# A two-layer encoder trunk on one core: weight splits held behind a norm, TensorE's own order kept at the end of an attention branch, and four weight splits of the second layer made ahead

## The chip, the cores and the metric

The kernel runs on one core of one Trainium2 chip. The metric is the device time of one execution in microseconds (us), the median over the runs. The engines are named as in the profile: PE is TensorE (PEld its weight loads), DVE is VectorE, ACT is ScalarE, POOL is GpSimd, SP is SyncE, which here only issues the weight transfers.

## The reference

`x` is 512 tokens of 1024 channels in float32. Two layers are computed; in each one

```python
h = hybrid_mixer(x, ...)                       # three branches A, B, C
x = layer_norm(ALPHA * x + h, ln1_g, ln1_b)
h = memory_cross_attention(x, mem, wq, wkv, wo)
x = layer_norm(ALPHA * x + h, ln2_g, ln2_b)
h = conv_ffn(x, w_up, conv_k, conv_b, w_down)  # gated MLP
x = layer_norm(ALPHA * x + h, ln3_g, ln3_b)
```

and the mixer is

```python
proj = x @ w_in                                # q, k, v of A and B, u and v of C, the gates
out_a = window_attention(...)                  # 8 heads of 64, banded
out_b = dense_block_attention(...)             # 8 heads of 64, all 512 keys
out_c = u * (W_s @ LN(v) + b)                  # C: spatial gating, u and v through gelu
gates = sigmoid(gate + b_gate)                 # 3 x 1024 channels
merged = sum over the branches of (branch @ w_branch) * gate
return merged @ w_mix_out
```

## The kernel before

**Products.** Each float32 operand of a projection is split into a high part (a copy to the type fp32r, `split_hi`, ACT, L132) and a low part (operand minus high part, `split_lo`, DVE, L137). A product is three matmuls, high by high, high by low and low by high (`mm3`, L143 to L145). `acc<-xT,w` is the form of most projections, with the transposed activations `xT` and a weight tile `w`.

**Weights.** The weights come in 292 transfers of 512 KB (`raw`, issued on SP in a fixed order). The class `Weights` splits each into a tile of the pool `w`, which has five slots (`N_WSLOT`). `pump` is called in and behind each step and starts a split as soon as `room` says that a slot is free: the one used five tiles before has had its last step. Tiles that `is_apart` names (the first two pairs of the MLP's up weights) have room of their own in a big tile, `upw`, and may be split from a step on that `W.open` gives.

**Steps and order.** `layer` appends steps in program order to a list. Afterwards they are run through one by one. A scheduler with a view over the whole program then decides in which order each engine gets its instructions; program order is a priority to it, no order. The steps of attention are urgent: they are written under a raised priority (`URGENT`). SP alone is under `tc.manual_schedule`, which keeps program order on the engines it names.

**Branch B.** Sixteen steps u = 0 to 15 (head u // 2, half u % 2 of the queries). I write S, T and PV for their three parts and S9.1 for the second of the two query blocks of step 9:

- S(u), `bS_step`: four matmuls `s<-Kt,Q` (L665), two for each query block; for each block the row maximum (DVE, L667), then the exponential into a slot of `ring` (ACT, L127); then a reciprocal (DVE, L672) and the scaling of both blocks (POOL, L674). `ring` has four slots for these, so S(u).1 writes where the transposes of T(u-2).1 read.
- T(u), `bT_step`: eight transposes `t<-ident,ring` (PE, L688), four a block; each block goes to `PTb` as a high part (ACT, L132) and a low part (DVE, L137).
- PV(u), `bPV_step`: eight matmuls `pv<-PTb,V` (L702). Behind an odd u the head's output is put together as `o` (ACT L127, then DVE L632), and behind each second head it is split into `brB` (ACT L132, DVE L137).

The program order is S(u), a filler, PV(u-2), T(u-1). A filler is a gate step (`gate_step`, 24 matmuls `acc<-xT,w`, then a tanh) or a branch projection (`br_step`, 12 matmuls `acc<-brA,w` or `acc<-brB,w`). In the program the fillers `fA` of branch A's gates and projections stand between the steps of B; those of branch B (`fB`) and the gates `gB[0]`, `gB[1]` stand behind them.

**Around the MLP's norm.** The cross-attention ends in `wo_step(0..3)`; each adds its half row to `x` (`residual`, L332, L335) and then the norm of a row block follows (`ln_finish`, L340 to L349), which `xT_step(t)` transposes (L323) and splits into `xT` (ACT L132, DVE L137). The first up projections (`up_half_step`, `pv<-xT,upw` and `acc<-xT,upw`) take them two row blocks at a time. At the end of a layer the same stands between `down_t_step(0..3)` and the next layer's `v_step`.

Of the kernel before, what the change touches and what calls it, by code (L numbers as in the profile page):

```python
# [11 lines left out]
F32R = mybir.dt.float32r  # L12
# [4 lines left out]
P = 128  # L17
# [6 lines left out]
NPAIR = 22  # L24
# [9 lines left out]
HALVED = (0, 1)  # L34
# [42 lines left out]
def encoder_kernel(ctx: ExitStack, tc: tile.TileContext, x_in, xt_in, mem_in, w_in, pp_in, ln_in, cln_in, ws_in, co_in, out):  # L77
# [27 lines left out]
    def acc_tile(n=512):  # L105
        return ps_acc.tile([P, 512], F32, tag="acc", name="acc")

    def pv_tile():
        return ps_pv.tile([P, 512], F32, tag="pv", name="pv")

    def s_tile():
        return ps_s.tile([P, 512], F32, tag="s", name="s")

    def t_tile(dt=F32):
        return ps_t.tile([P, 4, P], dt, tag="t", name="t")

    def big_tile(shape, dt, name):
        return big.tile(shape, dt, tag="big", name=name)

    def p_tile(shape=(P, 512), dt=F32, name="pt"):  # L120
        return sp.tile(list(shape), dt, tag="p", name=name)
# [42 lines left out]
    class Weights:  # L164
        def __init__(self):
            self.order, self.pos, self.last = [], {}, []
            self.raw, self.tiles, self.raw_order, self.sums = {}, {}, [], {}
            self.nl = self.ns = self.freed = self.nlo = 0
            self.late, self.done, self.first = [], set(), []
            self.slots, self.apart, self.open = [], {}, {}  # L170

        def plan(self, steps):
            for i, st in enumerate(steps):
# [72 lines left out]
                split_hi(t[:, 0, sl], r)  # L246
            return parts

        def is_apart(self, key):


            return key[1] == "up" and key[2] % NPAIR in HALVED

        def place(self, key):
            if not self.is_apart(key):
                self.slots.append(self.ns)
                return wpool.tile([P, 2, 1024], F32R, tag="w", name="w")
            l, i = key[0], key[2] % NPAIR
            if (l, i) not in self.apart:
                self.apart[l, i] = big_tile([P, 2, 2, 1024], F32R, "upw")  # L260
            return self.apart[l, i][:, key[2] // NPAIR]

        def room(self, step):
            key = self.order[self.ns]
            if self.is_apart(key):
                return step >= self.open[key[0]]
            n = len(self.slots)
            return n < N_WSLOT or self.last[self.slots[n - N_WSLOT]] <= step

        def pump(self, step):  # L270
            new = 0
            while self.ns < len(self.order) and self.room(step):
                self.split()
                new += 1
            while self.late and (len(self.late) > new or self.first[self.nlo] <= step + 1):
                self.late.pop(0)()
            while self.nl < len(self.raw_order) and self.nl < self.freed + self.ahead():
                self.load()
# [9 lines left out]
    W = Weights()  # L288
# [24 lines left out]
    def evac_T(dst_h, dst_l, ps):  # L313
        split_hi(dst_h, ps)
        split_lo(dst_l, ps, dst_h)

    def xT_step(t):
        def fn():
            for i in range(2):
                pt = t_tile()  # L320
                for j in range(4):
                    k = 4 * i + j
                    nc.tensor.transpose(pt[:, j, :], X[0][:, t, k * P:(k + 1) * P], ident)  # L323
                evac_T(xT[:, t, 0, 4 * i:4 * i + 4, :], xT[:, t, 1, 4 * i:4 * i + 4, :], pt)
            pump()
        return Step(fn)
# [3 lines left out]
    def residual(t, half, ps):  # L330
        xs = X[0][:, t, half * 512:(half + 1) * 512]
        nc.vector.scalar_tensor_tensor(out=xs, in0=xs, scalar=ALPHA, in1=ps, op0=ALU.mult, op1=ALU.add)  # L332
        if half == 0:
            ln_stats[t] = small.tile([P, 2, 6], F32, tag="bn", name="bn", bufs=4)
        nc.vector.bn_stats(out=ln_stats[t][:, half, :], in_=xs)  # L335
# [18 lines left out]
    def load_ln(l, i, tiles=None):  # L354
        if tiles is None:
            gb = kv_p.tile([P, 2, 2, 512], F32, tag="k", name="lngb")
            tiles = [[gb[:, j, hf, :] for hf in range(2)] for j in range(2)]
        for j in range(2):
            for hf in range(2):
                bcast_row(tiles[j][hf], ln_in[l, i, j, hf * 512:hf * 512 + 512].partition_broadcast(P))  # L360
        return tiles
# [16 lines left out]
    steps = []  # L378

    def add(fn, chunks=()):  # L380
        steps.append(Step(fn, chunks))

    def layer(l):
        K = lambda kind, c: (l, kind, c)
# [383 lines left out]
        def fillers(n, stage):  # L768
            f = []
            for m in range(8):  # L770
                f.append(gate_step(n, m))
                f.append(br_step(n, m, stage))
            return f
# [186 lines left out]
        def gs_make(k):  # L960
            g, v = g_view(k), gs_view(k)
            split_hi(v[:, 0, :], g)
            split_lo(v[:, 1, :], g, v[:, 0, :])
# [131 lines left out]
        def down_mm(half, c, t, ps):  # L1095
            w = W.get(K("down", half * 11 + c), 2, 512)
            sl = slice(t * P, (t + 1) * P)
            for j in range(2):
                k = 2 * c + j
                g = gs_view(k)  # L1100
                mm3(ps, g[:, 0, sl], g[:, 1, sl], w[:, 0, j, :], w[:, 1, j, :], k == 0, k == 2 * 11 - 1)
# [3 lines left out]
        def down_k_step(half, c):  # L1105
            def fn():
                if c == 0:
                    if half == 0:
                        R["dn", 0] = [s_tile(), s_tile(), pv_tile(), acc_tile()]
                        gt = kv_p.tile([P, DM], F32, tag="v", name="ln3g", bufs=2)  # L1110
                        bt = [p_tile(name="ln3b") for _ in range(2)]
                        R["ln"] = load_ln(l, 2, ([gt[:, :512], gt[:, 512:]], bt))
                    else:
                        R["dn", 1] = [acc_tile() for _ in range(2)] + [
                            t_tile().rearrange("p a b -> p (a b)") for _ in range(2)]
                if half == 0:
                    for k in range(2 * c + 2, min(2 * c + 4, NPAIR)):
                        gs_make(k)
                for t in range(NT):
                    down_mm(half, c, t, R["dn", half][t])  # L1120
                pump()
                if half == 0 and c == 10:
                    for t in range(NT):
                        residual(t, 0, R["dn", 0][t])
            return Step(fn, [K("down", half * 11 + c)])
# [19 lines left out]
        def st(s):  # L1145
            steps.append(s)
# [24 lines left out]
        fC, fA, fB = fillers(2, 0), fillers(0, 1), fillers(1, 2)  # L1171
        for nm, fl in (("a", fC), ("b", fA)):
            if nm == "b":
                st(q_step("b", 0))
                st(aT_step(15))
                st(q_step("b", 1))
                st(qT_step("b", 0))
                st(aPV_step(7))
                st(q_step("b", 2))
                st(qT_step("b", 1))  # L1180
                st(q_step("b", 3))
                st(qT_step("b", 2))
            for t in range(NT):
                st(kv_step(nm, t))
                if t == 0:
                    st(qT_step(nm, 3))
                else:
                    st(kT_step(t - 1))
            st(fl.pop(0))
            st(kT_step(3))  # L1190
            S_, T_ = (aS_step, aT_step) if nm == "a" else (bS_step, bT_step)
            for u in range(16):
                st(S_(u))
                if fl:
                    st(fl.pop(0))
                if nm == "a" and u >= 3 and u % 2 == 1:
                    st(aPV_step((u - 3) // 2))
                if nm == "b" and u >= 2:
                    st(bPV_step(u - 2))
                if u >= 1:  # L1200
                    st(T_(u - 1))
            for f in fl:
                st(f)
        gB = [f for f in fB[0::2]]
        pB = [f for f in fB[1::2]]
        fB = [gB[2]]
# [6 lines left out]
        st(bT_step(15))  # L1213
        st(gB[1])
        st(bPV_step(15))
        for f in fB[:6]:
            st(f)
        add(load_x)
        for f in fB[6:]:
# [29 lines left out]
        st(xS_step(3))  # L1249
        st(mv_step(1))  # L1250
        st(xT_att_step(2))
        W.open[l] = len(steps)
        st(xPV_step(0))
        st(xT_att_step(3))
        st(xPV_step(1))
# [9 lines left out]
        for i, (j, part) in enumerate(first):  # L1265
            st(up_half_step(j, part, 0))
            if i == 1:
                st(xT_step(2))
        st(xT_step(3))
        for t, (j, part) in enumerate(first):  # L1270
            st(up_half_step(j, part, 1))
# [12 lines left out]
        st(up_step(NPAIR - 1, 1))  # L1284
        for c in range(11):
            st(down_k_step(0, c))
        for c in range(11 - NTAIL):
            st(down_k_step(1, c))
        st(down_t_step(0))
# [8 lines left out]
    for l in range(NLAYER):  # L1298
        layer(l)
# [147 lines left out]
```

## Time and profile before

| | |
|---|---|
| median of 3 runs | 1813.61 us (1813.51 to 1814.2) |
| the profiled execution | 1813.72 us |
| its span, first to last instruction | 1811.8 us |
| mean granted TensorE clock | 0.993 of full |
| PE busy | 1773.7 us, 98% of the span |
| DVE busy | 1259.2 us, 69% |
| ACT busy | 826.5 us, 46% |
| POOL busy | 229.3 us, 13% |

The span is what the trace holds; 1.9 us lie around it. An engine's busy time is a mean over the whole kernel, so the stretches in which PE waits have to be looked for one by one.

### The profile page before, as it was taken

How to read it: one execution, taken by the hardware profiler on the slowest of the kernel's cores; microseconds unless marked ns; L12 is line 12 of the kernel's file. 1: busy time of each engine (PE TensorE's matmuls, PEld its weight loads, DVE VectorE, ACT ScalarE, POOL GpSimd, SP SyncE). 2: the span in 40 equal slices, each digit the busy share in tenths (PEclk: the TensorE clock that was granted, in tenths of full speed). 3: DMA queues.
4: the chain of work that ended last, by engine and by line, in shares of the span. 5: the costliest groups of instructions: out<-in, count | busy, mean ns of one | idle time of the engine just before them, and what ended most of it. 6: DMA issues, size and time to landing. Idle time of an engine off the chain costs nothing.

```text
span 1811.8 us, 25762 instructions
## 1 busy us (share of the span) xinstructions
PE 1773.7 (98%) x9928; PEld 1544.6 (85%) x9928; DVE 1259.2 (69%) x2092; ACT 826.5 (46%) x1426; POOL 229.3 (13%) x268
## 2 busy tenths in 40 slices
PE   8999999999999999999999999999999899999998
PEld 6888888878978999988788888888789799999886
DVE  6666856557687889983566668565575978889734
ACT  4355645532453555652133555455324435556510
POOL 1112423120110000000011124321201100000000
PEclk9999999999999999999999999999999999999999
DMA  6222221242430222353322222212333402223321
GB/s 237 94 70 72 70 93 57 64 142 93 158 119 22 94 82 106 115 171 98 102 102 95 92 71 71 82 59 82 124 115 122 128 24 93 95 84 136 134 90 47
DMA packets 51242, 176.73 MB, mean 98 GB/s; under 512 B 5680, under 2 KB 6192, under 8 KB 50864
## 3 DMA queue, kind: packets, MB, share of 16 engines
q1 hardware_dynamic: 44784, 158.86, 26.3%
q10 hardware_dynamic: 6336, 16.23, 2.6%
q8 instruction: 78, 1.28, 0.3%
q14 instruction: 44, 0.36, 0.1%
HBM read 170.87 MB, written 4.19 MB: 97 GB/s over the span
## 4 chain that ended last, share of the span: by engine, by line
PE 93%; DVE 5%; issue 1%; ACT 1%; DMA 0%; DVEq 0%; SPq 0%; ACTq 0%
PE acc L145 20%; PE acc L143 20%; PE acc L144 20%; PE t L1031 2%; PE t L1030 2%; PE t L1029 2%; PE pv L702 2%; PE acc L1031 2%; PE acc L1030 2%; PE acc L1029 2%; PE s L665 2%; DVE w L137 1%; PE t L688 1%; PE s L145 1%; PE s L144 1%; PE s L143 1%
## 5 line engine op out<-in xcount | busy, mean ns | idle before, releaser
L137 DVE TENSOR_TENSOR w<-raw,w 128x1024 fp32r<-128x1024 f32 (+1 forms) x332 | 387.8, 1178 | 222.2 <-ACT w L132 219.7
L132 ACT ACTIVATE w<-raw 128x1024 fp32r<-128x1024 f32 (+1 forms) x332 | 327.2, 995 | 416.3 <-PE acc L145 251.6
L143 PE MATMUL acc<-xT,w 128*128 128x512 f32 (+1 forms) x736 | 281.9, 384 | 0.0
L145 PE MATMUL acc<-xT,w 128*128 128x512 f32 (+1 forms) x736 | 281.6, 383 | 0.1
L144 PE MATMUL acc<-xT,w 128*128 128x512 f32 (+1 forms) x736 | 281.1, 382 | 0.0
L143 PE MATMUL acc<-w,xT 128*128 128x512 f32 (+1 forms) x432 | 156.0, 362 | 7.2 <-ACT w L132 6.7
L145 PEld LDWEIGHTS acc<-xT,w 128*128 128x128 f32 x736 | 138.4, 188 | 25.3 <-DVE w L137 0.5
L144 PEld LDWEIGHTS acc<-xT,w 128*128 128x128 f32 x736 | 138.6, 188 | 23.6
L143 PEld LDWEIGHTS acc<-xT,w 128*128 128x128 f32 x736 | 138.3, 188 | 23.3
L145 PE MATMUL acc<-w,xT 128*128 128x512 f32 (+1 forms) x432 | 156.7, 364 | 0.0
L144 PE MATMUL acc<-w,xT 128*128 128x512 f32 (+1 forms) x432 | 155.5, 361 | 0.5 <-DVE w L137 0.5
L297 POOL TENSOR_TENSOR rs<-ve,mhalf 128x1 f32<-128x1 f32 x32 | 29.7, 929 | 920.4 <-DVE ve L342 878.7
L143 PEld LDWEIGHTS acc<-w,xT 128*128 128x128 f32 x432 | 82.2, 190 | 19.3 <-ACT w L132 6.7
L144 PEld LDWEIGHTS acc<-w,xT 128*128 128x128 f32 x432 | 82.1, 190 | 12.9 <-DVE w L137 1.0
L145 PEld LDWEIGHTS acc<-w,xT 128*128 128x128 f32 x432 | 82.0, 190 | 11.5
L667 DVE TENSOR_REDUCE nm<-s 128x1 f32<-128x512 f32 x64 | 44.1, 688 | 63.9 <-PE s L665 63.8
L1031 PE MATMUL t<-S,w 128*128 128x256 f32 x288 | 81.5, 283 | 0.0
L1030 PE MATMUL t<-S,w 128*128 128x256 f32 x288 | 81.5, 283 | 0.0
L1029 PE MATMUL t<-S,w 128*128 128x256 f32 x288 | 81.5, 283 | 0.0
L600 POOL TENSOR_SCALAR ring<-ring,rsm 128x256 f32<-128x256 f32 (+1 forms) x64 | 41.8, 666 | 182.2 <-DVE rsm L598 142.2
L674 POOL TENSOR_SCALAR ring<-ring,rsm 128x512 f32<-128x512 f32 x64 | 44.5, 708 | 144.4 <-DVE rsm L672 131.0
L753 POOL TENSOR_TENSOR mg<-mg,ring 128x512 f32<-128x512 f32 x32 | 46.5, 1454 | 121.2 <-DVE ring L752 121.2
(308 smaller groups left out, 4401.7 us busy)
## 6 DMA issues: line engine op xcount, KB each, us to landing
raw<-in_w_dram SPq DMA_DIRECT2D x292, 512.0 KB, 3.6
lngb<-in_ln_dram ACTq DMA_DIRECT2D x16, 256.0 KB, 4.2
xraw<-in_xt_dram SPq DMA_DIRECT2D x4, 512.0 KB, 6.7
memr<-in_mem_dram ACTq DMA_DIRECT2D x2, 1024.0 KB, 4.8
x<-in_x_dram ACTq DMA_DIRECT2D x4, 512.0 KB, 7.4
x_keep<-x ACTq DMA_DIRECT2D x4, 512.0 KB, 2.6
x<-x_keep ACTq DMA_DIRECT2D x4, 512.0 KB, 5.0
out_dram<-x SPq DMA_DIRECT2D x8, 256.0 KB, 2.0
```

Of the source, the lines that this page charges most:

```text
L132: nc.scalar.activation(out, in_, AF.Copy, scale=scale)
L137: eng.tensor_tensor(out=out, in0=in_, in1=hi.bitcast(F32), op=ALU.subtract)
L143: nc.tensor.matmul(ps, lhsT=lh, rhs=rh, start=first, stop=False)
L144: nc.tensor.matmul(ps, lhsT=lh, rhs=rl, start=False, stop=False)
L145: nc.tensor.matmul(ps, lhsT=ll, rhs=rh, start=False, stop=last)
L600: nc.gpsimd.tensor_scalar(out=pr_t[qi], in0=pr_t[qi], scalar1=rs[:, qi:qi + 1], scalar2=0.0, op0=ALU.mult, op1=ALU.add)
L667: nc.vector.tensor_reduce(out=nm[:, qi:qi + 1], in_=ps, axis=AX.X, op=ALU.max, negate=True)
L674: nc.gpsimd.tensor_scalar(out=pr_t[qi], in0=pr_t[qi], scalar1=rs[:, qi:qi + 1], scalar2=0.0, op0=ALU.mult, op1=ALU.add)
L753: nc.gpsimd.tensor_tensor(out=mg, in0=mg, in1=tg, op=ALU.add)
L1029: nc.tensor.matmul(o, lhsT=wh, rhs=x(0, k), start=first and k == 0, stop=False, **f)
L1030: nc.tensor.matmul(o, lhsT=wh, rhs=x(1, k), start=False, stop=False, **f)
L1031: nc.tensor.matmul(o, lhsT=wl, rhs=x(0, k), start=False, stop=last and k == 3, **f)
```

## The change

The diff has three parts. First, `W.hold`: weight splits of the kinds `up` and `us` (the MLP's) that go to the five slots have no room before the step that stands at `xT_step(3)` in front of the MLP. Second, `pe_in_order`: from in front of S(14) of branch B until behind the second of `fB`, PE is under `manual_schedule` and so keeps program order there. Third, `apart_of` takes the place of `is_apart`: the four `v` weights of the second layer get room of their own too (the big tile is now called `wa`), and may be split from the step on at which the first layer's second down half begins.

```diff
-        def is_apart(self, key):
-            return key[1] == "up" and key[2] % NPAIR in HALVED
+        def apart_of(self, key):
+            l, kind, c = key
+            if kind == "up" and c % NPAIR in HALVED:
+                return (l, kind, c % NPAIR), c // NPAIR
+            if kind == "v" and l > 0:
+                return (l, kind, c // 2), c % 2
+            return None
...
         def room(self, step):
             key = self.order[self.ns]
-            if self.is_apart(key):
-                return step >= self.open[key[0]]
+            if self.apart_of(key) is not None:
+                return step >= self.open[key[:2]]
+            if key[1] in ("up", "us") and step < self.hold[key[0]]:
+                return False
             n = len(self.slots)
...
+    def pe_in_order():
+        pe_order.append(tc.manual_schedule(engines={mybir.EngineType.PE}))
+        pe_order[-1].__enter__()
...
             for u in range(16):
+                if nm == "b" and u == 14:
+                    add(pe_in_order)
                 st(S_(u))
...
         st(bPV_step(15))
-        for f in fB[:6]:
+        for f in fB[:2]:
+            st(f)
+        add(pe_free)
+        for f in fB[2:6]:
             st(f)
...
-        W.open[l] = len(steps)
+        W.open[l, "up"] = len(steps)
...
+        W.hold[l] = len(steps)
         st(xT_step(3))
...
+        W.open[l + 1, "v"] = len(steps)
         for c in range(11 - NTAIL):
             st(down_k_step(1, c))
```

In the changed kernel L665 is L681, L688 is L704 and L702 is L718; the norm's lines stand seven lower (L332 is L339).

**PE in the middle of branch B, first layer.** Before, the scheduler has filled each round of S, PV and T with gate matmuls; this is the piece from S(14) on:

```order
L665 MATMUL s<-Kt,Q 128x512
L688 MATMUL t<-ident,ring 128x128
L665 MATMUL s<-Kt,Q 128x512
L688 MATMUL t<-ident,ring 128x128 x2
L145 MATMUL acc<-xT,w 128x512
L143 MATMUL acc<-xT,w 128x512
L144 MATMUL acc<-xT,w 128x512
L145 MATMUL acc<-xT,w 128x512
L143 MATMUL acc<-xT,w 128x512
L144 MATMUL acc<-xT,w 128x512
```

In the change, the same engine some rounds earlier, where S(12) and S(13) stand with T(10) and PV(9); the rows `s` are S, `t` are T, `pv` are PV:

```order
L681 MATMUL s<-Kt,Q 128x512 x2
L704 MATMUL t<-ident,ring 128x128 x4
L681 MATMUL s<-Kt,Q 128x512 x2
L718 MATMUL pv<-PTb,V 128x256 x6
L704 MATMUL t<-ident,ring 128x128
L718 MATMUL pv<-PTb,V 128x256
L704 MATMUL t<-ident,ring 128x128
L718 MATMUL pv<-PTb,V 128x256
L704 MATMUL t<-ident,ring 128x128 x2
L681 MATMUL s<-Kt,Q 128x512 x2
L704 MATMUL t<-ident,ring 128x128 x4
```

The matmuls `acc<-xT,w` have gone from these rounds: from S9.1 to S14.1 five rounds of 20 instructions each follow one another with no filler in them, in both layers.

**PE at the end of branch B, first layer.** Before, the last transposes and the last two PV stand together, and the branch's own projections follow:

```order
L144 MATMUL acc<-brB,w 128x512
L145 MATMUL acc<-brB,w 128x512
L702 MATMUL pv<-PTb,V 128x256
L688 MATMUL t<-ident,ring 128x128 x4
L702 MATMUL pv<-PTb,V 128x256 x7
L688 MATMUL t<-ident,ring 128x128 x8
L702 MATMUL pv<-PTb,V 128x256 x16
L143 MATMUL acc<-brB,w 128x512 x2
```

In the change the rows from the last `acc<-brA,w` on are PV(11) with T12.1, PV(12), T(13), S(15), PV(13), T(14), and then the first gate step:

```order
L145 MATMUL acc<-brA,w 128x512
L718 MATMUL pv<-PTb,V 128x256 x6
L704 MATMUL t<-ident,ring 128x128
L718 MATMUL pv<-PTb,V 128x256
L704 MATMUL t<-ident,ring 128x128
L718 MATMUL pv<-PTb,V 128x256
L704 MATMUL t<-ident,ring 128x128 x2
L718 MATMUL pv<-PTb,V 128x256 x8
L704 MATMUL t<-ident,ring 128x128 x8
L681 MATMUL s<-Kt,Q 128x512 x4
L718 MATMUL pv<-PTb,V 128x256 x8
L704 MATMUL t<-ident,ring 128x128 x8
L143 MATMUL acc<-xT,w 128x512
```

The gate's 24 matmuls now stand between T(14) and PV(14), 24 more behind T(15) and 24 behind PV(15); the twelve `acc<-brA,w` ahead of PV(11) are the only fillers since S9.1.

**DVE around the MLP's norm, first layer.** `w` rows are low parts of weights, `x` and `bn` rows the norm, `xT` rows the transposed norm's low part. Before:

```order
L137 TENSOR_TENSOR w<-raw,w 128x1024
L137 TENSOR_TENSOR xT<-t,xT 128x512 x2
L340 BN_AGGR mv<-bn 128x2
L332 SCALAR_TENSOR_TENSOR x<-x,acc 128x512
L137 TENSOR_TENSOR w<-raw,w 128x1024
L332 SCALAR_TENSOR_TENSOR x<-x,acc 128x512
L137 TENSOR_TENSOR w<-raw,w 128x1024
L342 TENSOR_SCALAR ve<-mv 128x1
L346 SCALAR_TENSOR_TENSOR x<-x,mv,lngb 128x512 x2
L335 BN_STATS bn<-x 128x6
L137 TENSOR_TENSOR w<-raw,w 128x1024
L137 TENSOR_TENSOR xT<-t,xT 128x512 x2
```

In the change:

```order
L137 TENSOR_TENSOR w<-raw,w 128x1024
L137 TENSOR_TENSOR xT<-t,xT 128x512 x2
L347 BN_AGGR mv<-bn 128x2
L339 SCALAR_TENSOR_TENSOR x<-x,acc 128x512
L137 TENSOR_TENSOR w<-raw,w 128x1024
L339 SCALAR_TENSOR_TENSOR x<-x,acc 128x512
L137 TENSOR_TENSOR w<-raw,w 128x1024
L349 TENSOR_SCALAR ve<-mv 128x1
L353 SCALAR_TENSOR_TENSOR x<-x,mv,lngb 128x512 x2
L342 BN_STATS bn<-x 128x6
L137 TENSOR_TENSOR w<-raw,w 128x1024
L137 TENSOR_TENSOR xT<-t,xT 128x512 x2
```

Nothing moved here but line numbers: the same four `w` rows stand at the same places. PE's and ACT's rows of this stretch are the same too, and so are SP's.

## Rows read from the trace of the kernel before

**Rows 1.** The page: the span, and part 1.

```profile
span 1811.8 us, 25762 instructions
...
PE 1773.7 (98%) x9928; PEld 1544.6 (85%) x9928; DVE 1259.2 (69%) x2092; ACT 826.5 (46%) x1426; POOL 229.3 (13%) x268
```

**Rows 2.** PE's waits: line, waited for: us in total, times, longest.

```profile
PE pv L144 <- DVE xT L137: 8.8, 2, 4.4
...
PE acc L143 <- ACT brB L132: 4.1, 2, 2.1
...
PE pv L143 <- ACT xT L132: 2.6, 4, 1.0
PE t L323 <- DVE x L332: 1.5, 1, 1.5
...
PE pv L702 <- DVE o L632: 0.5, 2, 0.3
PE acc L143 <- DVE ring L752: 0.5, 2, 0.3
```

**Rows 3.** PE's timeline, end of branch B: start, us, instruction, [idle before <-releaser].

```profile
367.91 2.33 PE L702 MATMUL pv<-PTb,V 128*128 128x256 f32 x16 [0.26 <-DVE o L632]
372.30 0.73 PE L143 MATMUL acc<-brB,w 128*128 128x512 f32 x2 [2.06 <-ACT brB L132]
```

**Rows 4.** Windows: us, busy PE PEld DVE ACT POOL, PEclk, DMA share, GB/s.

```profile
1272.60:1276.00 3.40, 3.21 (x9) 2.23 (x8) 3.00 (x4) 2.38 (x3) 2.71 (x2) 0.50 0.10 19
...
372.30:375.70 3.40, 3.09 (x11) 1.95 (x12) 2.29 (x4) 1.06 (x1) 1.06 (x1) 1.00 0.00 0
545.30:548.90 3.60, 3.60 (x17) 3.60 (x18) 3.57 (x8) 0.00 (x0) 0.74 (x1) 0.50 0.00 0
```

**Rows 5.** PE's timeline, the rounds of S(14) and S(15).

```profile
348.27 0.75 PE L702 MATMUL pv<-PTb,V 128*128 128x256 f32 x5
...
352.52 0.62 PE L665 MATMUL s<-Kt,Q 128*128 128x512 f32 x2
352.97 0.88 PE L702 MATMUL pv<-PTb,V 128*128 128x256 f32 x6
...
354.28 0.71 PE L665 MATMUL s<-Kt,Q 128*128 128x512 f32 x2
354.82 0.60 PE L688 MATMUL t<-ident,ring 128*128 128x128 f32 x4
355.18 0.48 PE L143 MATMUL acc<-xT,w 128*128 128x512 f32 x1
```

**Rows 6.** ACT's timeline, the same rounds.

```profile
349.79 0.69 ACT L127 ACTIVATE ring<-s,nm 128x512 f32<-128x512 f32 x1 [5.54 <-PE t L688]
...
350.47 1.07 ACT L132 ACTIVATE PTb<-t 128x512 fp32r<-128x512 f32 x2
...
354.34 0.60 ACT L127 ACTIVATE o<-pv 64x512 f32<-64x512 f32 x1 [0.61 <-PE pv L702]
354.97 0.69 ACT L127 ACTIVATE ring<-s,nm 128x512 f32<-128x512 f32 x1
...
355.64 1.08 ACT L132 ACTIVATE PTb<-t 128x512 fp32r<-128x512 f32 x2
```

**Rows 7.** DVE's timeline, the same rounds.

```profile
351.11 1.27 DVE L137 TENSOR_TENSOR PTb<-t,PTb 128x512 fp32r<-128x512 f32 x2
...
356.55 1.27 DVE L137 TENSOR_TENSOR PTb<-t,PTb 128x512 fp32r<-128x512 f32 x2
```

**Rows 8.** DVE's timeline, the MLP's norm in the first layer.

```profile
543.38 1.21 DVE L137 TENSOR_TENSOR w<-raw,w 128x1024 fp32r<-128x1024 f32 x1
544.51 1.29 DVE L137 TENSOR_TENSOR xT<-t,xT 128x512 fp32r<-128x512 f32 x2
```

**Rows 9.** DVE's timeline, the seam between the layers.

```profile
902.73 2.35 DVE L137 TENSOR_TENSOR w<-raw,w 128x1024 fp32r<-128x1024 f32 x2
905.00 0.68 DVE L332 SCALAR_TENSOR_TENSOR x<-x,t 128x512 f32<-128x512 f32 x1
```

More of the change, by code (lines that the diff above doesn't have):

```diff
@@ L169, in __init__ @@
             self.late, self.done, self.first = [], set(), []
-            self.slots, self.apart, self.open = [], {}, {}
+            self.slots, self.apart, self.open, self.hold = [], {}, {}, {}
         def plan(self, steps):
@@ L247, in split_sums @@
             return parts
-        def is_apart(self, key):
-            return key[1] == "up" and key[2] % NPAIR in HALVED
+        def apart_of(self, key):
[5 more added lines that the diff above has]
+            return None
         def place(self, key):
-            if not self.is_apart(key):
+            ap = self.apart_of(key)
+            if ap is None:
                 self.slots.append(self.ns)
                 return wpool.tile([P, 2, 1024], F32R, tag="w", name="w")
[L258 to L261, printed above, removed]
+            if ap[0] not in self.apart:
+                self.apart[ap[0]] = big_tile([P, 2, 2, 1024], F32R, "wa")
+            return self.apart[ap[0]][:, ap[1]]
         def room(self, step):
             key = self.order[self.ns]
-            if self.is_apart(key):
-                return step >= self.open[key[0]]
+            if self.apart_of(key) is not None:
+                return step >= self.open[key[:2]]
+            if key[1] in ("up", "us") and step < self.hold[key[0]]:
+                return False
             n = len(self.slots)
@@ L381, in add, with pe_free @@
         steps.append(Step(fn, chunks))
+    pe_order = []
+    def pe_in_order():
+        pe_order.append(tc.manual_schedule(engines={mybir.EngineType.PE}))
+        pe_order[-1].__enter__()
+    def pe_free():
+        pe_order.pop().__exit__(None, None, None)
     def layer(l):
```

## The prediction

> **What bounds the kernel now.** I read the page first: PE is busy 1773.7 of 1811.8 us [rows 1], so about 38 us of PE idle are all that better timing could win. The list of PE's waits says where they lie [rows 2]: 8.8 us for DVE's `xT` (2 times, up to 4.4) and 2.6 for ACT's `xT`, around the MLP's norms; 4.1 us for `brB` (2 times), 0.5 for `o` and 0.5 for `ring`, at the end of branch B in each layer; 1.5 us for `x` at the seam between the layers. The timeline of branch B's end shows how the 4.1 arises [rows 3]: sixteen PV matmuls from 367.91, and then PE stands 2.06 us until the last head has gone through `o` and `brB`. Last I read the timelines of PE, ACT and DVE for the rounds before that end, to see what covers the softmax there.
>
> The profiled execution took 1813.72 us, 0.1 above the median; the sum is made on it. About 0.2% (3.6 us) is what a measurement of this kernel can tell from no change.
>
> **Part 1, the splits held behind the MLP's norm.** The order of DVE around the norm is the same before and after: four `w` splits among the rows of `x`, the last of them straight ahead of the `xT` pair for which PE waits. In the trace that split runs at 543.38 and the `xT` pair from 544.51 [rows 8]. The scheduler, with the whole program in view, puts the splits into the same holes although they are written later. So I count 0 for this part: the 8.8 and the 2.6 us stay.
>
> **Part 3, the second layer's `v` weights.** Their four splits move ahead into idle time of DVE and ACT. The seam stays: splits at 902.73 keep `x` waiting until 905.00 [rows 9], and in the order of the change splits of the next weights stand at those same places. So the 1.5 us stay, and 0 again; a reordering among the splits of the down phase, where they run ahead of their use, may be worth 0.5 us either way.
>
> **Part 2, program order on PE at branch B's end.** It does two things.
>
> It removes the end stall. `brB` is then needed only behind a gate of 24 matmuls, so the waits for `brB`, `o` and `ring` go: 4.1 + 0.5 + 0.5 = -5.1 us for both layers [rows 2].
>
> It takes the gates away from the rounds that come before it. The gates `gB` and the others stand behind S(14) in the program, and with PE in order they can no longer be pulled ahead. Five rounds, S9.1 to S14.1, are left with 20 instructions each. Such a round is in the trace, with filler behind it: from 352.52 to 355.18, 2.66 us of PE work [rows 5]. What stands against it is a chain that goes round once a round: PV(u-3) and the rest of T on PE, then the exponential of S(u).1 (ACT, in order, and its ring slot is free only when T has read it), then the high part of T's second block (ACT), its low part (DVE), then the next PV. Its length can be read at two places. Without `o`: PV(10) starts at 348.27, the exponential at 349.79, the high part at 350.47, the low part at 351.11 [rows 5 to 7]; the pair of low parts takes 1.27, so the first is done at about 351.75, and the length is 3.5 to 3.6 us. With an `o` copy of 0.60 us ahead of the exponential: PV(11) from 352.97, `o` at 354.34, exponential 354.97, high part 355.64, low part 356.55 and done at 357.2 [rows 5 to 7]: 4.1 from its second matmul, 4.2 from its first. I take 3.6 and 4.1. By the order of ACT in the change, three of the four periods between the five rounds carry an `o` or a `brB` copy, one carries none: 3 x 4.1 + 3.6 = 15.9 us, against 4 x 2.66 = 10.6 of work. That is 5.3 us of new waiting, in four pieces of 0.9 to 1.4.
>
> Behind the twelve `acc<-brA,w`, which cover the fifth, PV(12) follows on PV(11) and T12.1 directly. It is ready 4.1 us after PV(11), and PE has 1.3 us of work (352.97 to 354.28): 2.8 us. Then PV(13) follows on PV(12), T(13) and S(15). T13.0 ends 1.3 us behind PV(12)'s start; the high part (0.6), the low part (0.65), DVE's maximum of S15 between and the second low part (0.65 each) follow, which makes 3.9, while PE has 1.0 + 0.7 + 1.0 = 2.7 of work: 1.2 us. From there on a gate stands between, and the chain is covered. So per layer 5.3 + 2.8 + 1.2 = 9.3, and +18.6 us for both. Bounds: with every period at 3.5 the terms are 3.4, 2.3 and 0.5, which is 6.2 a layer and +12.4; the other bound is the clock's, below.
>
> **The clock.** PE's granted clock is full nearly throughout. After the second layer's 2 us wait for `brB`, 3.4 us run at 0.50, the lower of its two levels (1.2 GHz); after the same wait in the first layer they run at 1.00; after the 4.4 us wait 3.6 us run at 0.50 [rows 4]. So a wait of about 2 us sometimes brings the low clock and a longer one does. At half clock 3.4 us of work lose 1.7. The removed stall gives one such 1.7 back. The new 2.8 us, with shorter waits just before and behind it, I expect to cost it in both layers: 2 x 1.7 - 1.7 = +1.7.
>
> The Trainium skill ("TensorE: Matmul & The Clock Gate", section "HAM oscillation — how this bites in real kernels") says that a kernel whose groups of matmuls are separated by waits can find the clock lowered again for each group. The two `brB` waits agree with it in one case of two. [...]
>
> **Sum.** 1813.7 - 5.1 + 18.6 + 1.7 = 1828.9 us.
>
> **The rivals.**
>
> A, faster: the chain is no bound, because the exponentials run a round ahead of PV and the bare rounds follow PE's own pace. It decides at the period: if it is 2.66 us or less, no wait arises, the 5.1 and the 1.7 of the clock are saved and nothing is paid: 1813.7 - 6.8 = 1806.9. For it: S(u) is issued two steps ahead of PV(u). Against it: the ring has four slots, S(u).1 writes where T(u-2).1 reads, and both measured lengths are 3.5 and more. Chance 5%.
>
> B, the hold works at the norm: the four splits run later than the order lists them in time, and PE no longer waits for `xT`. That would give back 8.8 + 2.6 and the half-clock stretch behind each long wait, 2 x 1.8 us: 1828.9 - 15.0 = 1813.9, no change. For it: the split at 543.38 is 1.1 us of the 4.4. Against it: an engine takes its instructions in the order shown, and these rows are the same. Chance 4%.
>
> C, the clock falls in the bare rounds as well, as each has a wait of about 1 us. Then the PE part of each period, about 1.2 us from PV's second matmul to the end of T, takes twice as long, five times a layer: 5 x 1.2 = 6 us, and 1828.9 + 12 = 1840.9. For it: the half clock behind a 2 us wait. Against it: PE is still busy 2.66 of some 4 us, and the shortest wait in these rows that shows it is the 2.06. Chance 20%.
>
> **How the numbers follow.** My forecast holds 71%, A 5%, B 4%, C 20%. The predicted time is the likeliest's, 1828.9. Its low end is 1813.7 + 12.4 - 5.1 - 1.7 = 1819.3, with the short periods and no low clock at all; the range reaches up to C: 1819 to 1840. Faster by over 0.2% comes from A alone, 5%; within 0.2% from B, 4%; slower 91%.
>
> **What would show it.** In the profile after, the waits of PE for `xT` and the seam's for `x` stand as before; the wait for `brB` is gone; new waits of PE at the PV line, for DVE's or ACT's `PTb`, add up to about 18 us, with the longest (2 to 3 us) ahead of PV(12) in each layer. In the five rounds the starts of PV lie 3.6 to 4.1 us apart. The windows show whether the clock is at 0.50 behind PV(12) or in the rounds. The prediction is wrong if those starts lie 2.7 us apart, if PE's waits at the norm are shorter, or if the same gates' matmuls elsewhere get slower.

## The result and the profile after

The changed kernel took 1825.9 us (median of 4 runs, 1823.99 to 1827.68), the kernel before 1813.9 us (4 runs, 1813.51 to 1815.27). The ratio is 1.0065, 95% interval 1.0052 to 1.0077: 12 us slower, where 15 were forecast and 1819 to 1840 us was the range. The profiled execution took 1824.27 us with a span of 1822.5, which is 10.7 us above the span of before [rows 1].

First the list of PE's waits of the changed kernel (line, waited for: us in total, times, longest), beside [rows 2]:

```profile
PE pv L144 <- DVE xT L137: 8.8, 2, 4.4
...
PE pv L718 <- DVE o L648: 5.3, 2, 2.6
PE pv L718 <- DVE PTb L137: 4.1, 11, 0.6
...
PE pv L143 <- ACT xT L132: 2.6, 4, 1.0
PE s L681 <- ACT ring L127: 1.9, 5, 0.4
PE t L330 <- DVE x L339: 1.5, 1, 1.5
```

The 8.8, 2.6 and 1.5 us at the norm and the seam stand to the tenth as before: the held and the early splits moved nothing there. The waits for `brB` are gone, and three rows of branch B have come: 5.3 + 4.1 + 1.9 = 11.3 us against the 5.1 removed. That is 6.2 of the 10.7 us.

Nearly all of the rest is in PE's busy time, as part 1 of the page shows, beside [rows 1]:

```profile
PE 1777.7 (98%) x9928; PEld 1545.5 (85%) x9928; DVE 1258.9 (69%) x2092; ACT 827.1 (45%) x1426; POOL 228.8 (13%) x268
```

PE has the same 9928 matmuls and 4.0 us more of busy time. PE's timeline of the first layer (start, us, instruction, idle before and releaser) shows why. These are the PV of the five rounds without fillers, and then the stretch behind them:

```profile
311.74 0.88 PE L718 MATMUL pv<-PTb,V 128*128 128x256 f32 x6
...
315.70 0.86 PE L718 MATMUL pv<-PTb,V 128*128 128x256 f32 x5 [0.61 <-DVE PTb L137]
...
318.50 0.73 PE L681 MATMUL s<-Kt,Q 128*128 128x512 f32 x2 [0.37 <-ACT ring L127]
...
319.98 0.86 PE L718 MATMUL pv<-PTb,V 128*128 128x256 f32 x5 [0.33 <-DVE PTb L137]
...
323.64 0.86 PE L718 MATMUL pv<-PTb,V 128*128 128x256 f32 x5 [0.34 <-DVE PTb L137]
...
327.73 0.86 PE L718 MATMUL pv<-PTb,V 128*128 128x256 f32 x5 [0.26 <-DVE PTb L137]
...
337.97 2.56 PE L718 MATMUL pv<-PTb,V 128*128 128x256 f32 x8 [2.63 <-DVE o L648]
340.32 1.91 PE L704 MATMUL t<-ident,ring 128*128 128x128 f32 x8
341.88 2.06 PE L681 MATMUL s<-Kt,Q 128*128 128x512 f32 x4
...
344.47 1.11 PE L718 MATMUL pv<-PTb,V 128*128 128x256 f32 x7 [0.31 <-DVE PTb L137]
```

The reader should measure from start to start, not add up the idle times. The second matmul of PV(6) runs at 311.74 + 0.12 = 311.86, that of PV(10) at 327.73: four rounds in 15.87 us for 4 x 2.66 = 10.64 us of work, so 5.2 us lost, while the brackets between the two show 2.3 us. The difference lies in what the trace draws as busy. Of the rise of PE's busy time by 4.0 us with the same matmuls, one part is such waiting, the other work at half clock, below.

One thing in the section on the change is to be read otherwise: its `order` piece of before, given as the one from S(14) on, stands in the trace at S(9) and S(10) (308.18 and 316.40 us). It shows filled rounds all the same.

Ahead of PV(12) stand 2.63 us. Then eight transposes take 1.91 and the four matmuls of S(15) 2.06. The windows (us, busy PE PEld DVE ACT POOL, PEclk, DMA share, GB/s) show the clock there, in the first layer and then in the second:

```profile
337.50:344.20 6.70, 6.04 (x21) 4.98 (x21) 3.65 (x7) 1.82 (x3) 1.79 (x2) 0.50 0.25 78
1245.40:1248.80 3.40, 3.40 (x14) 2.88 (x12) 1.44 (x3) 1.17 (x2) 0.30 (x1) 0.50 0.06 24
```

Where the loss lies along the program is read at places that both traces have. The first transpose of the first norm, before:

```profile
445.40 0.82 PE L323 MATMUL t<-ident,x 128*128 128x128 f32 x6
...
1148.55 0.61 PE L665 MATMUL s<-Kt,Q 128*128 128x512 f32 x2
...
1345.34 0.93 PE L323 MATMUL t<-ident,x 128*128 128x128 f32 x7
```

and after, with the first S of the second layer's branch B between the two norms in both:

```profile
452.53 0.71 PE L330 MATMUL t<-ident,x 128*128 128x128 f32 x5
...
1155.81 1.07 PE L681 MATMUL s<-Kt,Q 128*128 128x512 f32 x4
...
1357.45 0.82 PE L330 MATMUL t<-ident,x 128*128 128x128 f32 x6
```

So +7.1 us arise in the first layer's branch B, +0.1 from there to the second layer's, and 12.1 - 7.3 = +4.8 in it. Of the 12.1 the end keeps 10.7. In the kernel before the 3.4 us from 1658.30 ran at the low clock and in the one after they did not, which is 1.7 us that no edit explains. After, the clock is 1.00 from 1669.00 to 1672.40; the window of before:

```profile
1658.30:1661.70 3.40, 3.40 (x18) 3.40 (x17) 3.40 (x8) 0.82 (x1) 0.00 (x0) 0.50 0.52 190
```

### The profile page after: what moved, and what is told of

It reads as the page before. It is cut to its first block, busy times and chain, and to the rows that moved or that the text cites. A ratio compares the mean times of both kernels' runs of the same rounds, so it can differ in the third digit from the quotient of the medians.

```text
span 1822.5 us, 25751 instructions
## 1 busy us (share of the span) xinstructions
PE 1777.7 (98%) x9928; PEld 1545.5 (85%) x9928; DVE 1258.9 (69%) x2092; ACT 827.1 (45%) x1426; POOL 228.8 (13%) x268
## 3 DMA queue, kind: packets, MB, share of 16 engines
HBM read 170.87 MB, written 4.19 MB: 96 GB/s over the span
## 4 chain that ended last, share of the span: by engine, by line
PE 90%; DVE 8%; issue 1%; ACT 1%; DMA 1%; DVEq 0%; SPq 0%; ACTq 0%
PE acc L145 20%; PE acc L144 20%; PE acc L143 20%; DVE w L137 2%; PE t L1047 2%; PE t L1046 2%; PE t L1045 2%; PE pv L718 2%; PE acc L1047 1%; PE acc L1046 1%; PE acc L1045 1%; PE t L704 1%; PE s L681 1%; PE s L143 1%; PE s L145 1%
## 5 line engine op out<-in xcount | busy, mean ns | idle before, releaser
L137 DVE TENSOR_TENSOR w<-raw,w 128x1024 fp32r<-128x1024 f32 (+1 forms) x328 | 383.6, 1179 | 240.1 <-ACT w L132 238.0
L132 ACT ACTIVATE w<-raw 128x1024 fp32r<-128x1024 f32 (+1 forms) x328 | 322.9, 994 | 396.9 <-PE acc L145 248.4
L143 PE MATMUL acc<-w,xT 128*128 128x512 f32 (+1 forms) x400 | 143.5, 360 | 6.6 <-ACT w L132 6.6
L145 PE MATMUL acc<-w,xT 128*128 128x512 f32 (+1 forms) x400 | 143.9, 361 | 0.0
L144 PE MATMUL acc<-w,xT 128*128 128x512 f32 (+1 forms) x400 | 143.1, 359 | 0.5 <-DVE w L137 0.5
L143 PEld LDWEIGHTS acc<-w,xT 128*128 128x128 f32 x400 | 76.2, 190 | 17.3 <-ACT w L132 6.6
L144 PEld LDWEIGHTS acc<-w,xT 128*128 128x128 f32 x400 | 76.1, 190 | 11.6 <-DVE w L137 1.0
L145 PEld LDWEIGHTS acc<-w,xT 128*128 128x128 f32 x400 | 76.1, 190 | 10.4
L132 ACT ACTIVATE xT<-t 128x512 fp32r<-128x512 f32 x40 | 22.2, 594 | 83.6 <-PE t L330 83.4
```

What stands on the lines that cost most here:

```text
L132: nc.scalar.activation(out, in_, AF.Copy, scale=scale)
L137: eng.tensor_tensor(out=out, in0=in_, in1=hi.bitcast(F32), op=ALU.subtract)
L143: nc.tensor.matmul(ps, lhsT=lh, rhs=rh, start=first, stop=False)
L144: nc.tensor.matmul(ps, lhsT=lh, rhs=rl, start=False, stop=False)
L145: nc.tensor.matmul(ps, lhsT=ll, rhs=rh, start=False, stop=last)
```

## The experiments

The kernel before ran beside each group: 1813.66, 1813.70 and 1813.39 us. Ratios are to it, with their 95% interval. None of these kernels leaves out work.

**e1, the second part alone.** The kernel before with `pe_in_order` and `pe_free` as in the change, nothing else.

> The kernel before with the second part alone (TensorE in program order from S(14) to behind the second of fB). Theory (the loss is the five rounds left without a filler and the uncovered PV(12)): as slow as the whole change, 1826 us (1824 to 1828), with the wait of 2.6 us ahead of PV(12) in both layers. Rival (the held or the early splits take part in the loss): clearly faster than the whole change, 1820 us or less.

1826.18 us (1825.01 to 1827.45, 5 runs), ratio 1.0069 (1.0056 to 1.0082). Its waits in branch B are 5.3, 4.8 and 1.9 us, nearly those of the change. The second part is the whole loss, as far as these runs can tell.

**e2, the first and third part alone.** The change without `pe_in_order` and `pe_free`.

> The change without its second part: the splits are held and the second layer's v weights split ahead, TensorE is free. Theory: no change, 1813.7 us (1812.5 to 1814.5), TensorE's waits of 4.42 us for xT at the MLP's norm and of 1.5 us at the seam as before. Rival (the splits take part in the loss): 1817 us or more. Rival (the hold gives something that the second part hides): 1811 us or less, with a shorter wait for xT.

1814.37 us (1812.87 to 1816.09, 11 runs), ratio 1.0007 (0.9998 to 1.0016): no change that can be told, and the waits for `xT` (8.8 us) and `x` (1.5 us) as before. Both rivals fall.

**e3, program order from the start of branch B.**

```diff
-                if nm == "b" and u == 14:
+                if nm == "b" and u == 0:
                     add(pe_in_order)
```

> The kernel before with the second part, but entered at S(0) in place of S(14): all of branch B is in program order, so each round keeps a filler of 12 or 24 matmuls, and the end stays as in the change. Theory (the missing fillers are the cost, program order as such is not): the end stall is saved (5.1 us, and up to 1.7 of clock), and only PV(13) behind S(15), which has no filler, waits about 1.2 us a layer: 1809 us (1807 to 1811). Rival (keeping program order is itself the cost, since TensorE then waits wherever the scheduler would have slipped something in): slower than the whole change, 1828 us or more.

1832.27 us (1831.91 to 1834.1, 4 runs), ratio 1.0105 (1.0092 to 1.0119). My number was wrong by 23 us, and on the rival's side. But the trace bears out the rival's reason at one place above all, and that one is not in the rounds. PE's timeline ahead of branch B, first layer:

```profile
230.80 0.54 PE L569 MATMUL t<-ident_r,ks 128*128 128x128 f32 x4 [0.78 <-DVE Q L526]
...
232.83 0.86 PE L569 MATMUL t<-ident_r,ks 128*128 128x128 f32 x4 [0.70 <-DVE Kt L570]
236.67 1.08 PE L569 MATMUL t<-ident_r,ks 128*128 128x128 f32 x4 [2.98 <-ACT ks L132]
238.54 0.80 PE L674 MATMUL s<-Kt,Q 128*128 128x512 f32 x1 [0.78 <-DVE Kt L570]
```

The fillers that had covered the preparation of K were now tied behind S(0), and PE stood 5.5 us there in each layer (0.78 + 0.25 + 0.70 + 2.98 + 0.78), with a mean clock of 0.62 of full from 230 to 240 us. Among the sixteen rounds that kept their fillers, only four show a wait at PV, of 0.42 to 0.74 us, and 1.05 us stand at PV(13), behind the round without one. The expectation had asked only who lacks fillers behind the point of entry, not who had used them ahead of it.

**e4, program order left ahead of the gates.**

```diff
+        add(pe_free)
         st(gB[0])
         st(bPV_step(14))
```

> The kernel before with the second part, but left ahead of gB[0]: only S(14) to T(14) are in program order, the gates behind them are free. By the order built, the five rounds from S9.1 to S14.1 are still without fillers, but PV(12) and PV(13) have gate matmuls ahead of them. Theory: the five rounds cost 5.2 us a layer, the stall of 2.6 us is gone and the end stall too: 1813.7 + 10.4 - 5.1, and 1.7 less for the clock, 1817 to 1819 us. Rival (the five rounds cost little, the 2.6 us and its low clock are the loss): 1811 us or less.

1816.92 us (1815.40 to 1817.35, 11 runs), ratio 1.0014 (1.0005 to 1.0023). The five rounds are there, with the same waits as in e1 (PV for `PTb` 3.1, S for `ring` 1.9 us), the waits ahead of PV(12) and for `brB` are not. So the five rounds with the end stall removed are worth +3.3 us (forecast: 10.4 - 5.1 - 1.7 = +3.6), and the other 9.3 us of e1 are the stretch from PV(12) to PV(15) with its clock.

That +3.3 meets the forecast is in part luck. At the places used above, e4's trace lies 1.2 us behind that of before at the first norm (446.56), 3.1 at the second layer's first S (1151.62) and 2.9 at the second norm (1348.21). Branch B itself costs only 1.2 us in the first layer and nothing in the second; most of the rest is a stretch at the low clock between the two, at which before ran at 1.00:

```profile
760.20:763.50 3.30, 3.30 (x18) 3.30 (x17) 3.30 (x8) 0.71 (x2) 0.00 (x0) 0.50 0.57 221
```

**e5, a hold that binds.** The hold of the change, and DVE in program order over the norm:

```diff
+        add(dve_in_order)
         st(wo_step(2))
         st(xT_step(0))
+        st(xT_step(1))
         st(wo_step(3))
-        st(xT_step(1))
...
             st(up_half_step(j, part, 1))
+            if t == 0:
+                add(dve_free)
```

> The kernel before with a hold that binds: the MLP's splits are held as in the change, DVE is kept in program order from wo_step(2) to behind the first up_half_step of the second two row blocks, and xT_step(1) stands ahead of wo_step(3). In the order built all four splits stand behind the norm. Theory (in the change DVE's order at the norm did not move, so the hold could do nothing; where it does move, the wait shrinks): by DVE's own work up to the second xT pair, that pair ends near 542.5 in place of 545.8, so the wait for xT falls from 4.4 us to 2 or 3, and some of the low clock behind it goes: 1809 us (1806 to 1811). Rival (the norm's own chain sets the wait, the splits are no part of it): 1813 us or more.

1811.13 us (1807.81 to 1813.51, 10 runs), ratio 0.9984 (0.9974 to 0.9993). The 4.4 us wait is gone altogether (0.2 is left of it, and 1.2 ahead of a transpose), more than I expected; but the time is above the forecast of 1809, since the splits come too late for what follows. From e5's list of PE's waits:

```profile
PE acc L143 <- DVE cv L982: 3.5, 2, 1.8
```

The 3.5 us for `cv` are new: five splits now run straight ahead of it.

**e9, the same without the hold.** e5 without `W.hold`; DVE's order and the moved `xT_step(1)` stay.

> e5 without the hold: the MLP's splits may start when a slot is free, as before, DVE is in program order from wo_step(2) on, and xT_step(1) stands ahead of wo_step(3). By the order built the four splits still stand behind the norm of the last row block, but ahead of the last two xT pairs. Theory (the order on DVE is what shortens the wait, the hold as such adds nothing): the wait for the second xT pair is as short as in e5 and the time is e5's 1811 us (1809 to 1813). Rival (the hold was needed): the wait of 4.4 us is back, 1813.7 us or more.

1805.91 us (1805.08 to 1807.14, 5 runs), ratio 0.9958 (0.9946 to 0.9971). Faster than e5 and than the 1811 us of the forecast: with DVE's order alone, the hold costs some 5 us. DVE's timeline at the norm shows the order that does it, beside [rows 8]:

```profile
540.21 1.29 DVE L137 TENSOR_TENSOR xT<-t,xT 128x512 fp32r<-128x512 f32 x2 [0.78 <-ACT xT L132]
...
547.13 4.63 DVE L137 TENSOR_TENSOR w<-raw,w 128x1024 fp32r<-128x1024 f32 x4
```

The second `xT` pair runs at 540.21 in place of 544.51, and the four splits stand between the norm of the last rows and the last two pairs, while PE works on the first two. The move of `xT_step(1)` and DVE's order were not run apart. Part of the gain is the clock behind the waits: the mean granted clock of e9's profiled execution is 0.997, that of before 0.993.

**e6, program order with a filler everywhere.** Gate steps of branch A in halves of 12 matmuls; six of the 24 pieces free ahead of S(0), then one in each round:

```diff
+        for m in range(8):
+            fA += [gate_half(0, m, 0), gate_half(0, m, 1), br_step(0, m, 1)]
...
-            st(fl.pop(0))
+            for _ in range(6 if nm == "b" else 1):
+                st(fl.pop(0))
             st(kT_step(3))
+            if nm == "b":
+                add(pe_in_order)
```

> The kernel before with TensorE in program order from S(0) to behind the second of fB as in e3, but with fillers for every stretch: each gate of branch A is cut into two halves of 12 matmuls, six of the 24 pieces stand free ahead of S(0) to cover the preparation of K, each of the sixteen rounds keeps one piece of 12, two more stand ahead of PV(14), and gB[0] and gB[1] cover PV(15) and brB. Theory (a round without a filler costs its chain of 3.6 to 4.1 us less 2.66; with 12 matmuls, 2.7 us, it costs nothing; what made e3 slow is the preparation of K alone): the end stall of 5.1 us goes and nothing comes in its place, 1808 us (1806 to 1811). Rival (program order as such costs time in the rounds): 1816 us or more, with waits at PV in most rounds.

1812.86 us (1812.21 to 1813.96, 10 runs), ratio 0.9995 (0.9986 to 1.0004): no change. From its list of PE's waits:

```profile
PE s L674 <- DVE Kt L570: 2.7, 2, 1.4
```

The end stall of 5.1 us is gone and the rounds cost little (2.5 us at PV over both layers, in 8 waits), but 2.7 us stand at the first S: 5.2 us came in its place. Against e1, the same kind of order with a filler in each round is 13 us faster. So keeping program order is not the cost; the missing fillers are.

**e7, six ring slots.** e1 with

```diff
+        def bpm_slot(i):
+            return ring()[:, i % 6, :]
...
         def tg_slot(n, m):
+            if n == 0:
+                return ring()[:, 6 + m % 2, :]
             return ring()[:, 4 + m % 4, :]
```

> e1 with six ring slots for branch B's exponentials in place of four (branch A's gates have two in place of four), so that the exponential of S(u).1 no longer waits for the transposes of T(u-2).1. By the order built there are still five to six rounds without a filler. Theory (the chain of a bare round runs through that slot): the chain loses the exponential, about 0.7 us, and the rounds fall from 3.6 to 4.1 us to about 3.0 to 3.5: 1820 us (1817 to 1823). Rival (the rounds are paced by the sum of ACT's or DVE's work in them): as slow as e1, 1825 us or more.

1825.20 us (1822.16 to 1827.23, 4 runs), ratio 1.0060 (1.0045 to 1.0075). The waits for `ring` are gone and those at PV have grown; e7's timeline of PE:

```profile
316.15 0.85 PE L711 MATMUL pv<-PTb,V 128*128 128x256 f32 x5 [1.32 <-DVE PTb L137]
...
320.58 0.76 PE L711 MATMUL pv<-PTb,V 128*128 128x256 f32 x5
...
323.49 0.86 PE L711 MATMUL pv<-PTb,V 128*128 128x256 f32 x5 [0.34 <-DVE PTb L137]
...
327.93 0.75 PE L711 MATMUL pv<-PTb,V 128*128 128x256 f32 x5
```

316.15 to 327.93 is 11.8 us for three rounds; in the change it was 12.0 (315.70 to 327.73). One round is now 2.9 us, the others 4.4. The windows of these rounds (same columns as above), for e1 and then for e7, fit the rival:

```profile
316.00:332.00 16.00, 13.90 (x82) 10.61 (x80) 12.49 (x24) 11.39 (x27) 5.60 (x9) 1.00 0.07 25
```

```profile
316.00:332.00 16.00, 14.20 (x88) 11.76 (x89) 13.65 (x26) 12.74 (x30) 5.48 (x8) 1.00 0.09 33
```

DVE was busy 78% in e1 and is busy 85% here, ACT 71% and 80%: the work of these two engines takes up most of a round, and a freer slot only moves the wait. That their work sets the pace is not shown. There is another candidate in e7's list of PE's waits:

```profile
PE pv L711 <- DVE o L641: 8.1, 6, 2.8
```

Two of the six stand ahead of PV(12), the others in the rounds (0.70 and 0.56 us in the first layer). `pv` has one buffer (`ps_pv`, `bufs=1`), so the first PV of a head waits until `o` of the head before has been read out of it. Neither a second buffer nor less work on DVE was tried.

**e8, e11 and e12, put together.** e8 is e5 and e6; e11 is e9 and e6, with seven pieces free ahead of S(0) and one ahead of PV(14); e12 is e11 with the hold.

> e5 and e6 together. Theory: both gains add up, 1813.7 - 4.5 - 5.5, 1804 us (1800 to 1807). Rival (either gives nothing): 1808 us or more.

> e6 with one more free piece of filler ahead of S(0) and one fewer ahead of PV(14), together with e9's order of DVE at the norm. Theory: e6's wait of 1.4 us a layer for Kt goes, the rest adds up as in e8: 1807 us (1805 to 1809). Rival (the piece is missed at the end as much as it helps at the start): 1809 us or more, with new waits at PV(14) or PV(15).

> e11 with the hold, so e8 with the one piece of filler moved. Theory: 1 to 2 us below e8's 1808.5 us: 1807 us (1805 to 1809), and equal to e11 if the hold adds nothing. Rival (the held splits cost time later, as e5's waits of 1.7 us for cv and 2.9 us for w do): 1 us or more above e11.

| | median us | runs | ratio to before |
|---|---|---|---|
| e8 | 1808.46 | 8, 1806.65 to 1812.72 | 0.9970 (0.9959 to 0.9980) |
| e11 | 1805.88 | 5, 1800.57 to 1807.08 | 0.9953 (0.9940 to 0.9965) |
| e12 | 1804.94 | 5, 1804.46 to 1806.42 | 0.9953 (0.9939 to 0.9966) |

All three beat both kernels. e8 fell short of the 1804 us that I expected, since e6 had gained nothing by itself. e11, e12 and e9 cannot be told apart, so the even fillers add nothing to DVE's order that these runs could show, and with them the hold costs nothing that they could show either. The plainest version that beats both kernels is e9: DVE in program order over the norm, and one step moved.

## Why the prediction was right, and where its terms were off

**Parts 1 and 3 count 0: right, and shown** by e2 and by PE's waits, which agree to the tenth. The hold sets only when a split is written in the program; a scheduler that sees the whole program puts it into the same hole. e5 and e9 show that the order on DVE was the thing to change. Rival B's price, 15 us for a hold that works, was too high: a hold that works gained 2.5 us (e5), and the order without it 7.5 (e9).

**The end stall goes: right** (no wait for `brB` is left), but its size, 5.1 us, was far too small; see the sum.

**Five rounds without fillers, 15.9 us for four periods: right in size** (15.87, in periods of 3.7 to 4.3), and rival A falls with it. The list of waits shows 11.3 us of new waits where I had named about 18 as a sign; the difference is drawn as busy. The reason that I gave is half right at most. I read one chain through PE, the exponential, the high and the low part, with the ring slot in it. e7 took the slot out of the chain and the rounds did not get shorter.

**PV(12), 2.8 us: right in size** (2.63 and 2.62), **but by another wait, so in part by luck.** I had read the chain through `PTb`, with 4.1 us from PV(11) to PV(12). The trace puts both waits to DVE's `o`, which must be read out of the one `pv` buffer first. PE's timeline, second layer, from PV(11) to PV(13):

```profile
1239.51 0.88 PE L718 MATMUL pv<-PTb,V 128*128 128x256 f32 x6
...
1243.69 0.36 PE L718 MATMUL pv<-PTb,V 128*128 128x256 f32 x1 [2.62 <-DVE o L648]
1244.38 1.10 PE L718 MATMUL pv<-PTb,V 128*128 128x256 f32 x7 [0.33 <-DVE PTb L137]
...
1249.39 1.10 PE L718 MATMUL pv<-PTb,V 128*128 128x256 f32 x7 [0.38 <-DVE PTb L137]
```

And DVE's, first layer, at the same place:

```profile
335.07 2.03 DVE L137 TENSOR_TENSOR w<-raw,w 128x1024 fp32r<-128x1024 f32 x1 [0.41 <-ACT w L132]
337.14 0.68 DVE L648 TENSOR_TENSOR o<-pv,o 64x512 f32<-64x512 f32 x1
...
337.93 0.67 DVE L137 TENSOR_TENSOR PTb<-t,PTb 128x512 fp32r<-128x512 f32 x1
```

A weight's low part of 2.03 us runs ahead of `o`, and `PTb` comes behind it: the second matmul of PV(12) starts 4.75 us after that of PV(11), not 4.1. My chain had no weight split in it. How long PV(12) would wait without this split was not run.

**PV(13), 1.2 us, and the low clock, 1.7, are one term.** I added them, but they overlap: at half clock T(13) and S(15) take longer on PE, and DVE's chain for PV(13) runs meanwhile. In the change PV(13) waits 0.31 and 0.38 us at the low clock; in e1's first layer, at full clock, it waits nearly what I had counted:

```profile
342.45 1.10 PE L711 MATMUL pv<-PTb,V 128*128 128x256 f32 x7 [1.04 <-DVE PTb L137]
```

From PV(12)'s first matmul to PV(13)'s second, 2.8 us of work (a round and one PV), stand 6.50 us in the change's first layer (337.97 to 344.47) and 5.70 in its second: 3.7 and 2.9 us lost, where 1.2 + 1.7 = 2.9 were forecast. In the first layer the low clock lasted twice as long as I had taken.

**The sum, +15.2, against +10.5 in the profiled execution and +12 in the medians.** Branch B, clock included, was to cost 9.3 - 2.6 + 1.7 = 8.4 us in the first layer and 6.7 in the second; it cost 7.1 and 4.8. The new loss was sized well, the removed one was not.

The new loss, from start to start: 5.2 us for the five rounds in each layer, 0.3 ahead of S14.1 in the first, 2.8 ahead of PV(12) (4.19 us from PV(11) less 1.36 of work), then the 3.7 and 2.9. That is 12.0 and 10.9 us, where 9.3 + 1.7 = 11.0 were forecast for each.

The removed loss I had read from idle time, 2.6 us a layer. The same piece of PE's timeline of before, in both layers, begins and ends so, around [rows 3]:

```profile
362.93 0.48 PE L143 MATMUL acc<-brB,w 128*128 128x512 f32 x1
...
376.26 0.39 PE L144 MATMUL acc<-brB,w 128*128 128x512 f32 x1
...
1261.59 0.47 PE L143 MATMUL acc<-brB,w 128*128 128x512 f32 x1
...
1276.20 0.40 PE L144 MATMUL acc<-brB,w 128*128 128x512 f32 x1
```

In between run 19 matmuls `acc`, 24 `pv` and 12 `t`, in 13.3 and 14.6 us. Their pace where nothing holds them up is 0.12 us a `pv` (above), about 0.1 a `t` (four in 0.36, [rows 5]) and 0.23 an `acc`, as twelve in the change take 2.74:

```profile
331.04 0.39 PE L143 MATMUL acc<-brA,w 128*128 128x512 f32 x1
...
333.78 0.88 PE L718 MATMUL pv<-PTb,V 128*128 128x256 f32 x6
```

So the piece is 8.4 us of work, an estimate from these rows, and the end of branch B lost 4.9 us in the first layer and 6.2 in the second, the low clock [rows 4] in it: 11.1 us, where 5.1 + 1.7 = 6.8 were forecast. Brackets show only what PE did not draw as busy. The new loss less the removed is 22.9 - 11.1 = 11.8 us, and 12.1 were measured at the second norm. What brings these down to 10.7 at the end is in the main the 1.7 us of clock behind the second layer's MLP, which the sum did not have.

**The clock.** It fell behind PV(12) as forecast, and not in the rounds: rival C falls, as the five rounds of e1 and e7 ran at 1.00 (windows above). The Trainium skill ("TensorE: Matmul & The Clock Gate", section "HAM oscillation — how this bites in real kernels") tells of a kernel whose clock is lowered again at each wait between groups of matmuls; those are waits for DMA that are longer than the ones between the rounds, so it does not decide on C. Behind the 2.6 us waits the change's trace agrees with it; at the 0.3 to 0.6 us between the rounds no run here shows it.

## What to carry to other kernels

A fixed order on one engine takes from the stretch ahead of it whatever the scheduler used to pull forward out of it: count the work that remains as cover in front of the section, not only the stall inside it. To keep low-priority work out of a critical chain, fix the order of the engine on which they compete; writing the work later in the program is no order where the scheduler sees all of it. Compare starts of the same instruction in two traces; sums of idle time miss waits that are drawn as busy, in the stall that is to be removed as in the one that comes.

## What the runs showed of the hardware

The low clock behind a wait of the same length comes in some places and not in others. In e1, whose order on PE in branch B is that of the change, the 4 us behind the first layer's wait of 2.63 us ran at 1.00 and those behind the second layer's at 0.50, each shown by its window:

```profile
338.00:342.00 4.00, 3.17 (x20) 2.57 (x20) 2.49 (x5) 1.26 (x4) 1.56 (x2) 1.00 0.33 124
1246.00:1250.00 4.00, 4.00 (x18) 3.71 (x18) 0.99 (x3) 1.19 (x2) 0.62 (x1) 0.50 0.16 67
```

In the change both layers had it. What it costs here is read from PV(12) to PV(13): 4.90 us in e1's first layer at full clock (337.55 to 342.45), 5.70 and 6.50 in the change, so 0.8 and 1.6 us, less than half of the stretch, as PE waits less meanwhile.

The four runs of the change lie in two pairs, 1823.99 and 1824.27, 1827.53 and 1827.68. Their mean granted clocks are 0.994 and 0.992, and 0.991 in both of the slower pair, so the lower clock goes with the longer time. Where in the kernel the slower pair lost it was not shown, since only one run of each kernel has a trace.
